# Gate and up as seven half-size block products, and the low part of weight tiles by an accumulating DMA

## Chip, cores and metric

One core of one Trainium2 chip runs the whole program in one launch. The metric is the device time of one execution in microseconds (us), median of several runs.

## What is computed

Two layers of a hybrid decoder for 512 prompt positions and 8 x 4 sample positions, 544 columns in all, in float32. In each layer four groups of heads read one projection of the normalised input, their outputs are joined by `w_out`, and a gated feed-forward part (FFN) follows. The change is about that part and about how all weights reach TensorE:

```
h2 = rmsnorm(x, p['norm2_g'])
gate, f_conv_new = causal_dwconv(st['f_conv'], h2 @ p['ffn_w_gate'], p['ffn_conv_w'])
x = x + (jax.nn.silu(gate) * (h2 @ p['ffn_w_up'])) @ p['ffn_w_down']
```

`D_MODEL` is 1024 (8 blocks of 128), `D_FF` is 2816 (22 blocks of 128), the convolution has width 3.

## The kernel before, in words

Activations lie with channels on the partitions and the 544 positions along the free dimension. A float32 product is made of three float32r products: a value is split into a high part (`hi`, a copy rounded to float32r) and a low part (`lo`, value minus `hi`), and `hi*hi`, `hi*lo` and `lo*hi` are added up in PSUM. `split` and `xsplit` do it for activations, `wprep` (L632) for weights.

**Weights.** `weights()` yields every weight tile in the order of use. `wload` loads the next one into a pool of two raw tiles (`wr`), a DMA on SP's queue (L630). `wprep` makes `wh` by a copy on ACT (L641) and `wl` by a subtraction on DVE (L643); both pools have three buffers. `wnext` keeps three tiles ready or in the making and hands out the oldest. A new `wh` can thus be written when PE has left a buffer that is three tiles older.

**Products.** `gemm` goes through the blocks of a tile: per block three products (high with high, weight high with activation low, weight low with activation high), each as two matmuls of 272 columns, so PE wants the low part of a tile at its fifth matmul. All matmuls are recorded at L417 by `mm`, which also keeps the planner's clock (`Order`): PE's order is fixed when the program is written, by that clock and the table `LAT` of waiting times for the side tasks; the order on the other engines is chosen by the scheduler of the tile framework.

**FFN.** `FGROUPS` cuts the 22 blocks of `D_FF` into groups of 6, 6, 6 and 4. For each block there is a gate product `pgt` and an up product `pup`, 8 blocks and 48 matmuls each. The gate result is multiplied by `rstd` (the norm), convolved (`conv`, a first pass on ACT at L694 and two on DVE), put through Silu on ACT, multiplied by `rstd` once more on POOL (L1584), then by the up result on DVE, and split into `hd`. POOL also copies the convolution's last columns to `sfo` (L1578, L1579). After a group come eight down products `pdn`, one per block of `D_MODEL`, that read the group's `hd` tiles and are added to `x`. The last two down products of the last layer are written out in `finale` as `pdl`, with one half of 272 columns at a time.

At the start of the program four weight tiles `w_tm` of 784 columns are the first that PE needs.

## Time and profile before

| | |
|---|---|
| median of 3 runs | 1375.87 us (1374.64 to 1376.35) |
| profiled execution, its own time | 1375.83 us |
| its span | 1374.0 us |
| PE busy | 1343.9 us, 98% |
| DVE, ACT, POOL busy | 777.2, 515.2, 292.2 us |
| DMA | 125.62 MB, mean 91 GB/s |
| granted TensorE clock, mean | 0.99 of 2.4 GHz |

The span runs from the first to the last instruction that the profiler saw; the execution's own time holds a little more around it. Busy times of different engines overlap. Durations of single matmuls overlap too, since they are pipelined: how fast PE goes is read from a run of them, as length over count.

### The profile page before, as it was taken

The page shows a single profiled execution, that of the slowest core. Times are in us where ns is not written, and L with a number is a line of the kernel's source. Part 1 is how long each engine was busy: PE and PEld are TensorE (multiplying, and loading weights), DVE is VectorE, ACT ScalarE, POOL GpSimd, SP SyncE. Part 2 cuts the span into 40 slices and gives each one's busy share as a digit, 9 for nine tenths or more (in the row PEclk, how much of TensorE's full clock was granted, in tenths as well). Part 3 has the DMA queues.
Part 4 walks back from the last instruction along what each step waited for, and adds up shares of the span by engine and source line. Part 5 has one row for each costly group of instructions (what it writes and reads, how often), then busy time and mean ns, then how long its engine had stood idle before and what let it go on. Part 6 is the DMA issues. An engine that isn't in the chain of part 4 may idle for free.

```text
span 1374.0 us, 30046 instructions
## 1 busy us (share of the span) xinstructions
PE 1343.9 (98%) x12982; PEld 1299.8 (95%) x12982; DVE 777.2 (57%) x1319; ACT 515.2 (37%) x852; POOL 292.2 (21%) x466
## 2 busy tenths in 40 slices
PE   8899999999999999999998999999999999999997
PEld 7888888999999999999998888989999999999997
DVE  5897944665445445435658977537444444444446
ACT  5446324443223223313534353335432332232234
POOL 2431220032103102203124311202320230121121
PEclk9899999999999999999999999999999999999999
DMA  6222241232232232232432222413223232322323
GB/s 224 89 83 72 82 133 43 82 113 77 81 106 79 76 107 80 74 106 67 140 120 79 78 82 62 138 52 87 92 81 89 93 85 80 98 89 71 103 68 96
DMA packets 48084, 125.62 MB, mean 91 GB/s; under 512 B 10144, under 2 KB 14432, under 8 KB 47824
## 3 DMA queue, kind: packets, MB, share of 16 engines
q1 hardware_dynamic: 47952, 123.70, 29.6%
q8 instruction: 102, 1.67, 0.5%
q14 instruction: 30, 0.25, 0.1%
HBM read 115.01 MB, written 8.67 MB: 90 GB/s over the span
## 4 chain that ended last, share of the span: by engine, by line
PE 88%; DVE 8%; issue 2%; ACT 1%; DMA 0%; DVEq 0%; SPq 0%; ACTq 0%
PE pup L417 19%; PE pgt L417 19%; PE pdn L417 19%; PE po L417 7%; PE ptm L417 2%; PE pj_b L417 2%; PE pj_z L417 2%; PE pj_u L417 2%; PE pj_h L417 2%; PE pj_cq L417 2%; PE pj_c L417 2%; PE p L417 2%; PE pj_v L417 1%; DVE wl L643 1%; DVE cacc L696 1%
## 5 line engine op out<-in xcount | busy, mean ns | idle before, releaser
L641 ACT ACTIVATE wh<-wr 128x1024 fp32r<-128x1024 f32 (+3 forms) x218 | 208.5, 957 | 502.0 <-PE pdn L417 177.2
L643 DVE TENSOR_TENSOR wl<-wr,wh 128x1024 fp32r<-128x1024 f32 (+3 forms) x218 | 246.2, 1129 | 24.2 <-ACT wh L641 18.3
L417 PE MATMUL pgt<-xl,wh 128*128 128x272 f32 x704 | 146.7, 290 | 0.0
L417 PE MATMUL pup<-xl,wh 128*128 128x272 f32 x704 | 146.7, 290 | 0.0
L417 PE MATMUL pup<-xh,wl 128*128 128x272 f32 x704 | 145.9, 289 | 0.0
L417 PE MATMUL pgt<-xh,wl 128*128 128x272 f32 x704 | 145.9, 289 | 0.0
L417 PE MATMUL pup<-xh,wh 128*128 128x272 f32 x704 | 145.9, 288 | 0.0
L417 PE MATMUL pgt<-xh,wh 128*128 128x272 f32 x704 | 145.9, 288 | 0.0
L417 PE MATMUL pdn<-hdl,wh 128*128 128x272 f32 x688 | 142.8, 289 | 0.0
L417 PE MATMUL pdn<-hdh,wh 128*128 128x272 f32 x688 | 142.4, 288 | 0.0
L417 PE MATMUL pdn<-hdh,wl 128*128 128x272 f32 x688 | 142.2, 288 | 0.0
L1600 DVE TENSOR_TENSOR xr<-xr,pdn 128x544 f32<-128x544 f32 x62 | 44.7, 721 | 142.0 <-PE pdn L417 141.8
L1578 POOL COPY sfo<-pbf 128x2 f32<-128x2 f32 x44 | 14.8, 336 | 517.9 <-DVE pbf L1576 517.9
L1576 DVE TENSOR_TENSOR pbf<-pgt,rstd 128x512 f32<-128x512 f32 x44 | 30.5, 693 | 148.3 <-PE pgt L417 142.9
L417 PEld LDWEIGHTS pgt<-xh,wh 128*128 128x128 f32 x704 | 110.8, 188 | 0.0
L417 PEld LDWEIGHTS pup<-xh,wh 128*128 128x128 f32 x704 | 110.8, 188 | 0.0
L417 PEld LDWEIGHTS pup<-xl,wh 128*128 128x128 f32 x704 | 110.7, 189 | 0.0
L417 PEld LDWEIGHTS pgt<-xl,wh 128*128 128x128 f32 x704 | 110.7, 189 | 0.0
L417 PEld LDWEIGHTS pgt<-xh,wl 128*128 128x128 f32 x704 | 110.7, 188 | 0.0
L417 PEld LDWEIGHTS pup<-xh,wl 128*128 128x128 f32 x704 | 110.7, 188 | 0.0
L417 PEld LDWEIGHTS pdn<-hdl,wh 128*128 128x128 f32 x688 | 108.1, 188 | 0.1
L417 PEld LDWEIGHTS pdn<-hdh,wl 128*128 128x128 f32 x688 | 108.1, 188 | 0.0
(523 smaller groups left out, 2680.0 us busy)
## 6 DMA issues: line engine op xcount, KB each, us to landing
wr<-w_g SPq DMA_DIRECT2D x44, 512.0 KB
wr<-w_u SPq DMA_DIRECT2D x44, 512.0 KB
wr<-w_ch SPq DMA_DIRECT2D x38, 512.0 KB
wr<-w_d SPq DMA_DIRECT2D x48, 384.0 KB
wr<-w_o SPq DMA_DIRECT2D x12, 384.0 KB
wr<-w_d SPq DMA_DIRECT2D x16, 256.0 KB
xr<-x_in SPq DMA_DIRECT2D x7, 544.0 KB
wr<-w_tm SPq DMA_DIRECT2D x8, 392.0 KB
```

Of the source, the lines that this page charges most:

```text
L417: nc.tensor.matmul(out, lhsT, rhs, **kw)
L641: act(hi, r, AF.Copy)
L643: tt(lo, r, hi.bitcast(F32), op=ALU.subtract)
L696: stt(acc[:, 0:out_n], pb[:, j:j + out_n], wcol[:, j:j + 1], acc[:, 0:out_n], op0=ALU.mult, op1=ALU.add)
L1576: tt(pb[:, 2:2 + SEQ], pflat(p, 0, SEQ), rstd[:, 0:SEQ], op=ALU.mult)
L1578: pool.tensor_copy(sfo[:, f, 0:2], pb[:, SEQ:SEQ + 2])
L1600: tt(xk(m), xk(m), pflat(p), op=ALU.add)
```

## The change

**Seven products for eight.** A gate and up pair is seen as a product of 2 x 2 blocks: outputs (gate, up) by halves of the 1024 input channels (4 blocks of 128 each), times those halves by halves of the 544 columns. Eight half-size block products become seven, on sums of weights and sums of activations. The first three pairs of a layer (`PLAIN`) stay as before, now with up right behind gate; in that time `Forms.make` builds the sums of activations, four times per layer: h2 times norm in `hn`, sums in `fu` and `fv`, and their high and low parts. The other 19 pairs run `seven`: chains of 4 blocks and 12 matmuls of 272 columns each, in the order `pA`, `pB`, `pD`, `pA`, `pD`, `pA`, `pC`. ACT copies parts of the chains' results out of PSUM between them (`sn`), DVE adds them up, and the second multiplication by `rstd` on POOL is gone for these pairs.

**Weight tiles of a pair.** Gate and up weights of a pair are loaded together into one raw tile `wg` of 2 x 1024 columns, a pool with one buffer. `wsums` makes `s31` and `s24` on DVE (one instruction of 1024 columns, two of 512). Four tiles go to PE: `g`, `s31`, `s24` (1024 columns each) and half of `u` (512 columns). The chains use g (twice), s31, s24 (twice), s31 again, u's half.

**Low part, for every weight tile of the program.** DVE's subtraction is replaced by: negate `hi` into `lo`, on DVE and ACT in turn (L729, L731 of the changed kernel), then a DMA that POOL issues and that adds the raw tile to `lo` (L732). There are 310 such DMAs.

**Order.** `FGROUPS` becomes 3, 5, 5, 5, 4. The down products of a group are spread behind the pairs of the next group, two behind each pair (three in the last group). Three times per layer a pair follows directly on a pair, at the borders of the groups. Several pools are merged into one, `slabs`; the sums for the second norm go from POOL to DVE.

```diff
-FGROUPS = [(0, 6), (6, 12), (12, 18), (18, 22)]
+FGROUPS = [(0, 3), (3, 8), (8, 13), (13, 18), (18, 22)]
+PLAIN = 3
...
+def _ffn_order():
+    o, todo = [], []
+    for f0, f1 in FGROUPS:
+        n = f1 - f0
+        for j, f in enumerate(range(f0, f1)):
+            o.append(("plain" if f < PLAIN else "seven", f, f0, f1))
+            k = -(-len(todo) // max(n - 1 - j, 1))
+            o += todo[:k]
+            todo = todo[k:]
+        o += todo
+        todo = [("down", m, f0, f1) for m in range(NK)]
+    return o + todo
+FFN_ORDER = _ffn_order()
...
-    hlp = ctx.enter_context(tc.tile_pool(name="hlp", bufs=28))
+    slabs = ctx.enter_context(tc.tile_pool(name="slabs", bufs=51))
...
+    wgu = ctx.enter_context(tc.tile_pool(name="wgu", bufs=1))
+    wsp = ctx.enter_context(tc.tile_pool(name="wsp", bufs=2))
...
-                pool.tensor_tensor(a, a, b, op=ALU.add)
+                self.es[0].tensor_tensor(a, a, b, op=ALU.add)
...
+    class Forms:
+        def __init__(self, src):
+            self.src, self.got, self.b11 = src, [], None
+        def make(self, kp):
+            h = []
+            for k in (kp, kp + NK // 2):
+                x, g = self.src(k)
+                t = n5("hn", T)
+                stt(t, x, g, rstd, op0=ALU.mult, op1=ALU.mult)
+                h.append(t)
+            (b11, b12), (b21, b22) = ((t[:, 0:HT], t[:, HT:T]) for t in h)
+            u, v = n5("fu", T), n5("fv", T)
+            n1, n2, t3, n4 = u[:, 0:HT], u[:, HT:T], v[:, 0:HT], v[:, HT:T]
+            tt(n1, b11, b12, op=ALU.subtract)
+            stt(n2, n1, -1.0, b22, op0=ALU.mult, op1=ALU.subtract)
+            tt(t3, b22, b12, op=ALU.subtract)
+            tt(n4, b21, n2, op=ALU.add)
+            j = kp % 2
+            if j == 0:
+                self.b11 = [nx("f1" + c, [128, T], F32R) for c in "hl"]
+            c_ = slice(HT * j, HT * j + HT)
+            act(self.b11[0][:, c_], b11, AF.Copy)
+            tt(self.b11[1][:, c_], b11, self.b11[0][:, c_].bitcast(F32), op=ALU.subtract)
+            sb, su, sv = split(h[1], "f2"), split(u, "f3"), split(v, "f4")
+            a, b = slice(0, HT), slice(HT, T)
+            self.got.append([[(t[0][:, s], t[1][:, s]) for t, s in
+                              ((self.b11, c_), (sb, a), (sb, b), (su, a), (su, b), (sv, a), (sv, b))]])
+        def parts(self):
+            return [[g[0][i] for g in self.got] for i in range(7)]
...
+    def chain(o, wt, k0, xs, start=True):
+        hi, lo = wt
+        n = len(xs)
+        for k in range(n):
+            xh, xl = xs[k]
+            for i, (w, x) in enumerate(((hi, xh), (hi, xl), (lo, xh))):
+                mm(o, w[:, k0 + k, :], x, start=start and k == 0 and i == 0, stop=k == n - 1 and i == 2,
+                   skip_group_check=not start)
+            yield 0.0
...
+            for kind, i, f0, f1 in FFN_ORDER:
+                if kind == "down":
+                    yield I["w_d"][l, i, :, f0:f1], f1 - f0, 128
+                elif kind == "plain":
+                    yield I["w_g"][l, i], NK, 128
+                    yield I["w_u"][l, i], NK, 128
+                else:
+                    yield I["w_g"][l, i], I["w_u"][l, i]
...
+        if len(x) == 3:
             r = wrp.tile([128, x[1], x[2]], F32, tag="wr", name="wr")
             nc.sync.dma_start(r, x[0])
-            wload_.append(r)
+        else:
+            r = wgu.tile([128, 2, NK, 128], F32, tag="wg", name="wg")
+            for i, src in enumerate(x):
+                nc.sync.dma_start(r[:, i], src)
+        wload_.append(r)
...
+    def wsums(gu):
+        K = NK // 2
+        g, u = gu[:, 0], gu[:, 1]
+        s31 = wsp.tile([128, NK, 128], F32, tag="ws", name="s31")
+        s24 = wsp.tile([128, NK, 128], F32, tag="ws", name="s24")
+        q = gu.rearrange("p a (h k) f -> p (a h) (k f)", h=2)
+        tt(s31.rearrange("p (h k) f -> p h (k f)", h=2), q[:, 0:4:3], bc(q[:, 2], 1, 2), op=ALU.add)
+        tt(s24[:, 0:K], g[:, 0:K], s31[:, K:NK], op=ALU.add)
+        tt(s24[:, K:NK], g[:, K:NK], s24[:, 0:K], op=ALU.add)
+        return [g, s31, s24, u[:, K:NK]]
...
+        if not wsplit_:
+            if not wload_:
+                wload()
+            if not wload_:
+                return
+            r = wload_.pop(0)
+            wsplit_.extend([r] if len(r.shape) == 3 else wsums(r))
+        r = wsplit_.pop(0)
         nk, w = r.shape[1], r.shape[2]
         hi = whp.tile([128, nk, w], F32R, tag="wh", name="wh")
         act(hi, r, AF.Copy)
         lo = wlp.tile([128, nk, w], F32R, tag="wl", name="wl")
-        tt(lo, r, hi.bitcast(F32), op=ALU.subtract)
+        turn[0] ^= 1
+        if turn[0]:
+            ts(lo, hi.bitcast(F32), -1.0, None, op0=ALU.mult)
+        else:
+            act(lo, hi.bitcast(F32), AF.Copy, scale=-1.0)
+        pool.dma_start(out=lo, in_=r, accum_op=ALU.add)
         wready.append((hi, lo))
...
-            nrm = Norm((pool, pool))
+            nrm = Norm((dve, dve))
...
+            def seven(f):
+                B11, B21, B22, N1, N2, T3, N4 = fm.parts()
+                K = NK // 2
+                a_ = ps("pA", [128, HT])
+                b_ = psa.tile([128, HT], F32, tag="pa1", name="pB")
+                d_ = psa.tile([128, HT], F32, tag="pa0", name="pD")
+                sn = pd.tile([128, 4, HT], F32, tag="d5", name="sn")
+                pb, dec = gate_in(f)
+                n = SEQ - HT
+                wg_ = wnext()
+                yield from chain(a_, wg_, 0, B11)
+                act(sn[:, 0], a_, AF.Copy)
+                yield from chain(b_, wg_, K, B21)
+                tt(pb[:, 2:2 + HT], b_, sn[:, 0], op=ALU.add)
+                w31 = wnext()
+                yield from chain(d_, w31, K, N1)
+                act(sn[:, 1], d_, AF.Copy)
+                w24 = wnext()
+                yield from chain(a_, w24, 0, N2, start=False)
+                act(sn[:, 2], a_, AF.Copy)
+                yield from chain(d_, w24, K, B22, start=False)
+                tt(pb[:, 2 + HT:2 + SEQ], d_[:, 0:n], sn[:, 2, 0:n], op=ALU.add)
+                tt(dec[:, :, 2:6], bs(d_[:, n:HT]), bs(sn[:, 2, n:HT]), op=ALU.add)
+                sl = gate_out(f, pb, dec)
+                yield from chain(a_, w31, 0, T3, start=False)
+                act(sn[:, 3], a_, AF.Copy)
+                up = n5("up", T)
+                stt(up[:, HT:T], a_, -1.0, sn[:, 1], op0=ALU.mult, op1=ALU.subtract)
+                c_ = psmm("pC")[:, 0:HT]
+                yield from chain(c_, wnext(), 0, N4)
+                tt(up[:, 0:HT], c_, sn[:, 3], op=ALU.subtract)
+                tt(sl, sl, up, op=ALU.mult)
+                hid[f] = split(sl, "hd")
...
+            for kind, i, f0, f1 in FFN_ORDER:
+                if kind == "plain":
+                    for step in plain(i, i == 0):
+                        yield step
+                    if i < 2:
+                        fm.make(2 * i)
+                        fm.make(2 * i + 1)
+                    continue
...
```

On ACT, in the FFN of layer 0, a stretch of one pair and the tiles behind it. Before (`wh` is a weight tile's high part, `hdh` that of a hidden block, `cacc` the convolution, `sl` Silu):

```order
L641 ACTIVATE wh_4642<-wr_4640 128x768
L694 ACTIVATE cacc_4631<-pbf_4624,prm0_125 128x560
L1582 ACTIVATE sl_4635<-cacc_4631 128x512
L1583 ACTIVATE sl_4635<-cacc_4631 128x32
L641 ACTIVATE wh_4702<-wr_4700 128x768
L499 ACTIVATE hdh_4695<-sl_4635 128x544
```

After (`wl` is the negation, `sn` a copy out of PSUM; `wh_5667` and `wh_5726` are the two down tiles, `wg_5750` the next pair's raw tile):

```order
L725 ACTIVATE wh_5616<-s24_5532 128x1024
L731 ACTIVATE wl_5618<-wh_5616 128x1024
L1696 ACTIVATE sn_5612<-pA_5609 128x272
L725 ACTIVATE wh_5647<-wg_5528 128x512
L1701 ACTIVATE sn_5612<-pD_5611 128x272
L1704 ACTIVATE sn_5612<-pA_5609 128x272
L725 ACTIVATE wh_5667<-wr_5665 128x640
L783 ACTIVATE cacc_5701<-pbf_5613,prm0_122 128x560
L731 ACTIVATE wl_5669<-wh_5667 128x640
L725 ACTIVATE wh_5726<-wr_5724 128x640
L1710 ACTIVATE sn_5612<-pA_5609 128x272
```

The negation of `s24` and of the first down tile now stand on ACT, the latter behind the convolution's first pass.

On POOL in the same stretch, before (`sfo` and `pbf` are the convolution's edges):

```order
L1578 COPY sfo_3909<-pbf_5106 128x2
L1579 COPY sfo_3909<-pbf_5106 128x16
L687 MEMSET pbf_5236 128x2
L689 COPY pbf_5236<-stf_3907 128x8x2
L1584 TENSOR_TENSOR sl_5117<-sl_5117,rstd_104 128x544
```

After:

```order
L732 DMA wl_5618<-s24_5532 128x1024
L732 DMA wl_5649<-wg_5528 128x512
L1656 COPY sfo_3941<-pbf_5613 128x2
L1657 COPY sfo_3941<-pbf_5613 128x16
L732 DMA wl_5669<-wr_5665 128x640
L776 MEMSET pbf_5835 128x2
L778 COPY pbf_5835<-stf_3939 128x8x2
L732 DMA wl_5728<-wr_5724 128x640
L732 DMA wl_5760<-wg_5750 128x1024
```

Six DMAs per pair and its two down tiles stand in POOL's queue, with the copies of the convolution's edges between them.

On PE, the border between a pair and the first down product after the change (a name with DMASW is the end of an accumulating DMA):

```order
L436 MATMUL pC_5723<-f4l_4312,wh_5647 128x272
L436 MATMUL pC_5723<-f4h_4311,wl_5649 128x272
L436 MATMUL pdn_5749<-hdh_4587,wh_5667 128x272 [waits DVE_49,Activation_49]
L436 MATMUL pdn_5749<-hdh_4587,wh_5667 128x272
L436 MATMUL pdn_5749<-hdl_4588,wh_5667 128x272 x2
L436 MATMUL pdn_5749<-hdh_4587,wl_5669 128x272 [waits DMASW5_49]
L436 MATMUL pdn_5749<-hdh_4587,wl_5669 128x272
```

The fifth matmul of a down product waits for the accumulating DMA into its low part, where it waited for DVE.

## Rows read from the trace of the kernel before

**Rows 1.** The page, its first part: busy time, share of the span, instructions.

```profile
span 1374.0 us, 30046 instructions
PE 1343.9 (98%) x12982; PEld 1299.8 (95%) x12982; DVE 777.2 (57%) x1319; ACT 515.2 (37%) x852; POOL 292.2 (21%) x466
```

**Rows 2.** The chain that ended last, merged: start us, length us, what.

```profile
304.05 6.08 PE pup L417 x48
...
358.77 36.37 PE pdn L417 x288
...
1357.46 4.53 PE pdl L417 x36
```

**Rows 3.** Windows, FFN of layer 0: first two gate and up groups.

```profile
core 0: us, PE busy (x) PEld busy (x) DVE busy (x) ACT busy (x) POOL busy (x), PEclk, DMA share, GB/s
285.00:359.00 74.00, 74.00 (x587) 74.00 (x586) 36.78 (x50) 29.46 (x43) 22.42 (x32) 1.00 0.26 84
395.00:468.00 73.00, 73.00 (x579) 73.00 (x578) 35.42 (x47) 24.70 (x36) 20.32 (x30) 1.00 0.28 83
```

**Rows 4.** Lines by form, PE and its weight loads, one product of three.

```profile
L417 PE MATMUL pup<-xh,wl 128*128 128x272 f32 x704 | 145.9, 289 | 0.0
L417 PEld LDWEIGHTS pup<-xh,wl 128*128 128x128 f32 x704 | 110.7, 188 | 0.0
```

**Rows 5.** Lines by form, ACT and DVE: shapes, count | busy us, mean ns | idle before.

```profile
L641 ACT ACTIVATE wh<-wr 128x1024 fp32r<-128x1024 f32 x132 | 139.6, 1058 | 313.9 <-PE pgt L417 142.1 <-PE pdn L417 63.9 <-PE pup L417 27.3
L641 ACT ACTIVATE wh<-wr 128x768 fp32r<-128x768 f32 x60 | 50.7, 846 | 156.0 <-PE pdn L417 105.4 <-PE pgt L417 26.0 <-PE pup L417 18.7
L694 ACT ACTIVATE cacc<-pbf,prm 128x560 f32<-128x560 f32 x44 | 33.7, 765 | 7.0 <-DVE pbf L1577 4.5
L641 ACT ACTIVATE wh<-wr 128x512 fp32r<-128x512 f32 x18 | 11.4, 632 | 26.6 <-PE pgt L417 8.7 <-PE pup L417 6.2 <-PE pdn L417 5.7
...
L643 DVE TENSOR_TENSOR wl<-wr,wh 128x1024 fp32r<-128x1024 f32 x132 | 167.9, 1272 | 19.8 <-ACT wh L641 13.9
L643 DVE TENSOR_TENSOR wl<-wr,wh 128x512 fp32r<-128x512 f32 x18 | 12.3, 684 | 0.0
```

**Rows 6.** Timeline, 394.9 to 397.6 us, one weight tile on ACT, DVE and SP's queue.

```profile
394.93 1.06 ACT L641 ACTIVATE wh<-wr 128x1024 fp32r<-128x1024 f32 x1 [3.49 <-PE pdn L417]
...
396.02 1.23 DVE L643 TENSOR_TENSOR wl<-wr,wh 128x1024 fp32r<-128x1024 f32 x1
...
397.27 0.33 SPq L630 DMA_DIRECT2D wr<-w_g  x1
```

**Rows 7.** Windows of half a microsecond behind that issue; last columns: DMA share, GB/s.

```profile
398.00:398.50 0.50, 0.50 (x6) 0.50 (x5) 0.00 (x0) 0.00 (x0) 0.00 (x0) 1.00 0.56 66
...
399.50:400.00 0.50, 0.50 (x6) 0.50 (x5) 0.00 (x0) 0.00 (x0) 0.00 (x0) 1.00 1.06 434
400.00:400.50 0.50, 0.50 (x6) 0.50 (x5) 0.00 (x0) 0.00 (x0) 0.00 (x0) 1.00 0.15 57
400.50:401.00 0.50, 0.50 (x6) 0.50 (x5) 0.00 (x0) 0.00 (x0) 0.00 (x0) 1.00 0.00 0
```

**Rows 8.** Lines, POOL: the same copy in the FFN and elsewhere.

```profile
L1579 POOL COPY sfo<-pbf 128x16 f32<-128x16 f32 x44 | 44.2, 1003 | 0.0
...
L1503 POOL COPY sbo<-pbb 128x16 f32<-128x16 f32 x4 | 0.8, 195 | 0.0
```

**Rows 9.** Timeline, 5.8 to 8.0 us: the program's first weight tile.

```profile
5.89 0.84 ACT L641 ACTIVATE wh<-wr 128x784 fp32r<-128x784 f32 x1
...
6.77 0.98 DVE L643 TENSOR_TENSOR wl<-wr,wh 128x784 fp32r<-128x784 f32 x1 [0.51 <-ACT wh L641]
...
7.80 0.45 PE L417 MATMUL ptm<-wl,xh 128*128 128x392 f32 x1 [0.57 <-DVE wl L643]
```

**Rows 10.** Windows at 50 to 60 us, columns as in rows 3.

```profile
50.00:55.00 5.00, 0.74 (x4) 0.74 (x4) 4.90 (x15) 2.46 (x4) 1.85 (x6) 0.77 0.13 49
55.00:60.00 5.00, 5.00 (x24) 5.00 (x24) 4.19 (x10) 2.35 (x5) 0.00 (x0) 0.50 0.33 107
```

**Rows 11.** The page, DMA queues: packets, MB, share of 16 engines' span.

```profile
q1 hardware_dynamic: 47952, 123.70, 29.6%
```

More of the change, by code (lines that the diff above doesn't have):

```diff
@@ L451, in n5, with nx @@
         return p5.tile([128, w], F32, tag="w5", name=nm)
-    def nx(nm, shape):
-        return px.tile(shape, F32, tag="x5", name=nm)
+    def nx(nm, shape, dt=F32):
+        return slabs.tile(shape, dt, tag="s5", name=nm)
     def ncc(nm, shape):
@@ L459, in ny @@
     def ny(nm, shape):
-        return pyy.tile(shape, F32, tag="y5", name=nm)
+        return nx(nm, shape)
     def ps(nm, shape):
@@ L496, in split @@
     def split(src, nm):
-        hi = hlp.tile([128, T], F32R, tag="hl", name=nm + "h")
-        lo = hlp.tile([128, T], F32R, tag="hl", name=nm + "l")
+        hi, lo = nx(nm + "h", [128, T], F32R), nx(nm + "l", [128, T], F32R)
         act(hi, src, AF.Copy)
@@ L543, in xsplit @@
     def xsplit(x, g):
-        hi = hlp.tile([128, T], F32R, tag="hl", name="xh")
-        lo = hlp.tile([128, T], F32R, tag="hl", name="xl")
+        hi, lo = nx("xh", [128, T], F32R), nx("xl", [128, T], F32R)
         act(hi, x, AF.Copy, scale=g)
@@ L615, in weights @@
                 yield I["w_o3"][l, m], NK, 128
[L616 to L621 removed]
+            for kind, i, f0, f1 in FFN_ORDER:
[6 more added lines that the diff above has]
+                    yield I["w_g"][l, i], I["w_u"][l, i]
     wgen = weights()
[L624 removed]
+    wload_, wsplit_, wready, turn = [], [], [], [0]
     def wload():
         x = next(wgen, None)
[L628 removed]
+        if x is None:
+            return
+        if len(x) == 3:
             r = wrp.tile([128, x[1], x[2]], F32, tag="wr", name="wr")
             nc.sync.dma_start(r, x[0])
[L631 to L638 removed]
+        else:
[13 more added lines that the diff above has]
+        return [g, s31, s24, u[:, K:NK]]
+    def wprep():
+        if not wsplit_:
+            if not wload_:
+                wload()
+            if not wload_:
+                return
+            r = wload_.pop(0)
+            wsplit_.extend([r] if len(r.shape) == 3 else wsums(r))
+        r = wsplit_.pop(0)
         nk, w = r.shape[1], r.shape[2]
@@ L786, in gates @@
         L.beta, L.nbeta, L.gg, L.ex, L.bec = beta, nbeta, gg, ex, bec
-        L.oT = [lv.tile([128, T], F32, tag=f"oT{pr}", name=f"oT{pr}") for pr in range(2)]
+        L.oT = [nx(f"oT{pr}", [128, T]) for pr in range(2)]
         od.mark(f"gates{l}", 1.0)
     def halves(x):
-        h = hlp.tile([128, SEQ], F32R, tag="hl", name="hvh")
-        lo = hlp.tile([128, SEQ], F32R, tag="hl", name="hvl")
+        h, lo = nx("hvh", [128, SEQ], F32R), nx("hvl", [128, SEQ], F32R)
         act(h, x, AF.Copy)
@@ L1442, in main @@
             cq = L.cq = pd.tile([128, 2, T], F32, tag="d5", name="cq")
-            ck = L.ck = lv.tile([128, T], F32, tag="ck", name="ck")
+            ck = L.ck = nx("ck", [128, T])
             rope = pd.tile([128, 2, T], F32, tag="d5", name="rope")
@@ new lines, in main, with gate_in, gate_out @@
+            hid = {}
+            fm = Forms(lambda k: (xk(k), P(l, "n2g", k, k + 1)))
+            def gate_in(f):
+                pb = n5("pbf")
+                return pb, conv_in(pb, 3, stf[:, f])
+            def gate_out(f, pb, dec):
+                pool.tensor_copy(sfo[:, f, 0:2], pb[:, SEQ:SEQ + 2])
+                pool.tensor_copy(sfo[:, f, 2:18].rearrange("p (b s) -> p b s", b=DB), dec[:, :, 4:6])
+                acc, accd = conv(pb, 3, P(l, "fcw", 3 * f, 3 * f + 3), 560)
+                sl = n5("sl", T)
+                act(sl[:, 0:SEQ], acc[:, 0:SEQ], AF.Silu)
+                act(bs(sl[:, SEQ:T]), accd, AF.Silu)
+                return sl
@@ new lines, in plain @@
+            def plain(f, first):
+                p = psmm("pgt")
+                yield from gemm(p, wnext(), xs)
+                pu = psmm("pup")
+                gu = gemm(pu, wnext(), xs)
+                if first:
+                    for _ in range(4):
+                        yield next(gu)
+                    nrm.finish()
+                pb, dec = gate_in(f)
+                tt(pb[:, 2:2 + SEQ], pflat(p, 0, SEQ), rstd[:, 0:SEQ], op=ALU.mult)
+                tt(dec[:, :, 2:6], bs(pflat(p, SEQ, T)), bs(rstd[:, SEQ:T]), op=ALU.mult)
+                sl = gate_out(f, pb, dec)
+                pool.tensor_tensor(sl, sl, rstd, op=ALU.mult)
+                yield 0.0
+                yield from gu
+                tt(sl, sl, pflat(pu), op=ALU.mult)
+                hid[f] = split(sl, "hd")
+                yield 0.0
@@ new lines, in main @@
+            for kind, i, f0, f1 in FFN_ORDER:
[6 more added lines that the diff above has]
+                    continue
+                if kind == "seven":
+                    yield from seven(i)
+                    continue
+                m, last = i, f1 == NF
+                hd = [hid[f] for f in range(f0, f1)]
+                if last and l + 1 == depth and m >= NK - 2:
+                    if m == NK - 2:
+                        yield from finale(xk, xr, nnrm, hd)
+                    continue
+                p = psmm("pdn")
+                yield from gemm(p, wnext(), hd)
+                tt(xk(m), xk(m), pflat(p), op=ALU.add)
+                if last:
+                    if l + 1 < depth:
+                        nx_xs.append(xsplit(xk(m), P(l + 1, "n1g", m, m + 1)))
+                    nnrm.feed(m, xk(m))
+                    if l + 1 == depth:
+                        act(xk(m), xk(m), AF.Copy, scale=fng[:, m:m + 1])
+                yield 0.0
```

70 lines of the change are left out of this document (5 added, 65 removed).

## The prediction

> **What bounds the kernel now.** I read the page's first part, then the chain of waits, the windows by stage, the lines by form, and last the timeline around one weight tile. PE is busy for 1343.9 of 1374.0 us [rows 1], and the chain is a string of PE pieces: a gate or up product of 48 matmuls takes 6.08 us, eight down products of 36 take 36.37 us [rows 2]. Both give 0.1267 us per matmul. In the feed-forward (FFN) stretches PE never stops, while DVE, ACT and POOL are busy for 35.42, 24.70 and 20.32 of 73 us [rows 3]. So in the FFN only two things count: how many matmuls PE issues, and whether a weight tile is ever late.
>
> A weight tile is made well ahead. Its first copy on ACT starts when PE leaves the buffer three tiles back, at 394.93; the subtraction on DVE is done at 397.25 [rows 6]. PE wants the tile two tiles later, 12.2 us after the start. 2.3 us are used, so some 10 us are in hand.
>
> **What is saved.** A gate and up pair is 96 matmuls now. Seven chains of 4 blocks x 3 products are 84. Each matmul already loads its own weights (704 loads for 704 matmuls [rows 4]), so a chain that uses a weight for one half only loses nothing there, and the pace holds where a product fills a single 272-wide tile: 36 matmuls in 4.53 us [rows 2]. Twelve matmuls fewer are 1.52 us, for 19 of 22 pairs in 2 layers: 38 x 1.52 = 58 us less. That gain I count as certain.
>
> **What is added: a transfer inside the making of every tile.** The low part was one DVE instruction (1272 ns for 1024 columns [rows 5]). It becomes a negated copy, on DVE and ACT in turn, and an accumulating DMA that POOL issues. No row of before shows such a DMA. Call D the time from POOL reaching it to the low part being usable, for 1024 columns.
> - Lower bound: a plain load of the same 524 KB. SP issues it at 397.27 [rows 6]; bytes flow from about 398.2, at up to 434 GB/s, and only 28 KB are left after 400.0 [rows 7]: landed at 400.1, D = 2.8 (0.9 lead, 1.9 body). No reason excludes less, so that is a rival below.
> - Upper bound: that load twice over, 5.6, since source and destination are both read.
> - I take the load plus one more reading at its peak rate, 524 KB / 434 GB/s = 1.2: D = 4.0. It is nearest to the row of the load, with the one thing added that the operation must do. By columns (lead 0.9, rest in proportion): 2.8 for 640, 2.5 for 512, 3.3 for 784.
>
> The Trainium skill ("DMA: Bandwidth & Descriptors", section "Anatomy of one DMA — SWDGE (gpsimd) path") fits a DMA issued from GpSimd as 2.0 us plus bytes over 436e3, which is an estimate of 3.2 us for this tile. With it in place of 4.0 the sum below would be 1435; no run here shows an accumulate, so it stays beside the sum.
>
> **Where D lands on the path.** Three buffers remain, but a pair of 84 matmuls now uses four tiles (g, s31, s24, half of u), so a tile lasts PE 1.52 or 3.04 us instead of 6.08. The look-ahead shrinks to the following, per pair and the two down products behind it. PE needs 10.64 us for the pair and 3.80 for each 5-block down product.
> - *s24.* Its buffer comes free when the down product ahead of the pair ends. PE reaches its low part after three chains and two matmuls: 4.56 + 0.25 = 4.8 us. The work: ACT copy 1.06, ACT negation 1.06 (same form [rows 5]), 0.1 of hand-overs, D 4.0: 6.2. **Late by 1.4 us.**
> - *First down tile.* It takes the buffer that s24 leaves after its second chain; PE is there after two more chains and four matmuls: 3.04 + 0.51 = 3.55 us. The work: copy of 640 columns 0.74 (between 632 ns for 512 and 846 for 768), then on ACT's queue the convolution's 0.77 stands before the negation of 0.74 [rows 5], 0.1, and 2.8: 5.15. **Late by 1.6 us.**
> - *Covered.* s31 has two down products' end and two chains ahead (3.80 + 3.04 + 0.25 = 7.1 us against 1.06 + 1.27 + 4.0); u's half four chains (6.3 against 3.8); the second down tile the whole first one; the next g both down products.
>
> So a pair saves 1.52 and waits 3.0: +1.5 us, for 32 of the 38 pairs: **+48 us**.
>
> *Pair directly behind pair* (3 per layer, at the group borders). The raw tile for g and u has one buffer. Its next load can start only when the accumulate of u's half has read it: two chains 3.04, copy 0.63, negation 0.68 (512 columns at the DVE price of a two-input op [rows 5], an upper bound), hand-over 0.1, 2.5: 6.95 us into the pair. The load takes 2.8, copy and negation 2.1, D 4.0, 0.1: 16.0, where PE wants it at 10.9. Late by 5.1, then s24 by 1.4: 6.5 less 1.5 saved, +5.0 x 6 = **+30 us**.
>
> *Start.* The first low part follows its copy by 0.98 us on DVE and PE takes it at once [rows 9]. It will be 0.85 for the negation plus 3.3: +3.2 on each of the first three tiles, before PE has anything else: **+10 us**.
>
> *New operands.* Four times per layer DVE and ACT make the sums of activations: per time one half-width and three full copies on ACT, some 2.4 us, about 10 per layer, queued before the copies of weight tiles while only plain pairs cover them. Their lead of 10 us absorbs most; I take half, 5 per layer: **+10 us**.
>
> At nothing: DVE's three weight sums per pair (1272 + 2 x 684 ns [rows 5]) lie between load and use in slack of the down products; the removed multiplication by the norm on POOL, the removed subtractions and the moved norm sums were off the chain. If DVE lost its slack, s31 would be late next.
>
> **Sum.** The profiled execution took 1375.83 us, its span 1374.0; the median of the runs is 1375.87, so the two agree. The 58 us are inside the net figures: 48 + 30 + 10 + 10 = +98, **1474 us**. With D = 2.8 the same steps give -13 + 11 + 7 + 10 = +15, 1391. With 5.6: 131 + 53 + 13 + 10 = +207, 1583.
>
> **Rivals.**
> 1. *The accumulate is quick and the saving stays: faster.* The point is D = 2.5; below it the waits cost less than 1.52 per pair. At D = 2.0 s24 is on time, the first down tile late by 0.4, pair behind pair by 2.0: -36 + 3 + 5 + 10 = -18, 1358. For it: no byte goes to HBM, and rate peaks at 434 GB/s. Against: a load with no second operand takes 2.8 [rows 6, 7]. Chance 0.09.
> 2. *POOL is held up at the issue.* POOL's copy of 16 columns takes 1003 ns in the FFN, 195 ns for the same shape elsewhere [rows 8]: something on the other engines holds it for 0.8 us. If an issue is held for half of that, 0.4 at each wait: 0.8 x 32 + 1.2 x 6 = +33, 1507. Chance 0.12. The Trainium skill ("SBUF — State Buffer", section "SBUF: two separate sides") names a shared DVE and GpSimd port that a DVE op of the two-port kind, as the negation may be, takes for a whole instruction, and says GpSimd can then not write descriptors; the 0.8 us fits a lock, while no row shows one on an issue.
> 3. *The DMA engines become the bound.* A pair with two down products loads 1.70 MB and accumulates 2.49 MB. 123.70 MB in 29.6% of the span [rows 11] is 304 GB/s while busy: 5.6 us for loads, and at two passes 16.4 for accumulates, 22.0 against the 21.2 of my sum, close to the edge already. At two and a half passes, 26: +4.9 x 32 = +157 more, 1631. For peak-rate bytes (434) the total is 15.4, which speaks against. Chance 0.10.
> 4. *Gain and waits cancel*, D near 2.5: 1376. Chance 0.02.
>
> The forecast has the remaining 0.67. A further cost in the range only: after 4.3 us of idle PE in 5 the granted clock showed 0.50, the 1.2 GHz level, over the next window [rows 10]; waits of 1.5 us are short of that, those of 5 are not.
>
> **How the numbers follow.** The range runs from 1390 (D = 2.8) to 1600 (D = 5.6 and a little clock): it leaves out rivals 1, 3 and 4, 0.21 together. Slower by over 0.2% (2.75 us, about what a measurement of this kernel can tell from no change): forecast and rivals 2 and 3, 0.89; within it rival 4, 0.02; faster rival 1, 0.09.
>
> **What would show it.** Right: PE's matmuls drop by 38 x 12 and its busy time by some 55 us, yet PE idles in the FFN on low parts, 1 to 2 us at each pdn behind a pC and at the third chain of a pair, 5 at the g of a pair behind a pair; ACT and POOL lie on the chain. An accumulate that lands under 2.5 us, or an FFN stretch without idle PE, makes it wrong; so does DMA busy near 1.0 in FFN windows (rival 3).

## The result, and the profile after

The changed kernel takes **1880.8 us** (1874.3 to 1884.0, 4 runs) against 1376.0 on the same chip: 1.367 times the time of before, 95% interval 1.363 to 1.370. The forecast was 1474, its range ended at 1600. The direction was right, the size was not. In an execution now and then the chip falls into a slower state; the ratios leave such executions out, which matters for one of the four of `before_acc16k` below.

The page of the changed kernel, parts 1 to 4, beside [rows 1] and [rows 11] of before:

```profile
span 1878.1 us, 30986 instructions
...
PE 1457.5 (78%) x12526; PEld 1371.8 (73%) x12526; DVE 819.6 (44%) x1596; ACT 774.3 (41%) x1283; POOL 428.3 (23%) x722
...
q0 software_dynamic: 44640, 130.63, 36.1%
q1 hardware_dynamic: 50256, 123.70, 21.1%
...
PE 34%; DMA 28%; issue 21%; DVE 8%; ACT 6%; POOL 2%; SPq 0%; DVEq 0%; POOLq 0%; ACTq 0%
```

PE has 456 matmuls fewer (12526 for 12982), and yet is busy 114 us longer. It also stands still for 421 us of the span instead of 30. The chain, a string of PE pieces before [rows 2], is now 34% PE, 28% DMA and 21% "issue" (time in which an engine waited for nothing that the profile shows). The windows of the FFN of layer 0, columns as in [rows 3], show both losses at once:

```profile
480.00:530.00 50.00, 33.34 (x216) 32.04 (x217) 17.20 (x30) 19.75 (x31) 10.36 (x18) 0.86 0.56 121
530.00:580.00 50.00, 36.97 (x244) 35.45 (x242) 19.26 (x32) 20.51 (x31) 9.54 (x16) 0.86 0.65 152
```

PE idles for a quarter to a third of the time, its granted clock falls from 1.00, the 2.4 GHz level, to a mean of 0.86 between that and 1.2 GHz, and the DMA engines are far from full (0.56, 0.65). What does PE wait for? Its waits, longest groups (us in total, times, longest):

```profile
PE pdn L436 <- DMA wl<-wr: 118.1, 53, 4.8
PE pA L436 <- DMA wl<-s: 111.6, 38, 4.7
PE pA L436 <- DMA wl<-wg: 67.4, 30, 5.5
PE pD L436 <- DMA wl<-s: 41.3, 26, 2.4
```

Low parts, all of them: of down tiles (`pdn`), of s24 (`pA` from `s`), of g (`pA` from `wg`) and of s31 (`pD`). The prediction had named the first two, g only where a pair follows directly on a pair, and had called s31 covered; the half of u, called covered too, is not in the list. POOL's timeline for one pair and its two down tiles (start us, length, instruction, idle time before it and what ended it) tells why:

```profile
536.26 0.87 POOL L732 DMA_DIRECT2D wl<-wr  x1 [3.92 <-DVE up L1712]
541.43 0.87 POOL L732 DMA_DIRECT2D wl<-wg  x1 [4.30 <-issue]
546.83 0.87 POOL L732 DMA_DIRECT2D wl<-s  x1 [4.53 <-issue]
551.55 0.86 POOL L732 DMA_DIRECT2D wl<-s  x1 [3.85 <-issue]
556.30 0.89 POOL L732 DMA_DIRECT2D wl<-wg  x1 [3.89 <-issue]
...
561.56 0.87 POOL L732 DMA_DIRECT2D wl<-wr  x1 [1.61 <-ACT wl L731]
...
566.60 0.89 POOL L732 DMA_DIRECT2D wl<-wr  x1 [3.93 <-DVE up L1712]
```

An issue takes POOL 0.87 us, and then POOL sits for some 4 us before the next although nothing in the trace holds it ("issue"). The chain shows the transfer of 551.55:

```profile
551.55 4.44 DMA wl<-s
```

It lands at 555.99, and the next one starts at 556.30. By the landing times in the trace not one of the 310 accumulates is issued before the one ahead of it has landed; the closest follows 0.31 us behind. Six of them make the period: 536.26 to 566.60, 30.3 us, where the prediction had 21.2. Of it 26.6 us are transfers; for 2.0 us, from 559.53 to 561.56, the queue is empty until ACT has negated the first down tile.

### The profile page after: what moved, and what is told of

It reads as the page before. It is cut to its first block, busy times and chain, and to the rows that moved or that the text cites. A ratio compares the mean times of both kernels' runs of the same rounds, so it can differ in the third digit from the quotient of the medians.

```text
span 1878.1 us, 30986 instructions
## 1 busy us (share of the span) xinstructions
PE 1457.5 (78%) x12526; PEld 1371.8 (73%) x12526; DVE 819.6 (44%) x1596; ACT 774.3 (41%) x1283; POOL 428.3 (23%) x722
## 3 DMA queue, kind: packets, MB, share of 16 engines
q0 software_dynamic: 44640, 130.63, 36.1%
## 4 chain that ended last, share of the span: by engine, by line
PE 34%; DMA 28%; issue 21%; DVE 8%; ACT 6%; POOL 2%; SPq 0%; DVEq 0%; POOLq 0%; ACTq 0%
DMA wl<-wr 9%; DMA wl<-s 9%; PE pdn L436 7%; PE pD L436 4%; PE pA L436 4%; DMA wg<-w_u 3%; ACT wh L725 3%; POOL wl L732 2%; PE pup L436 2%; DMA wl<-wg 1%; PE pj_z L436 1%; PE pj_b L436 1%; DMA wr<-w_d 1%; PE po L436 1%; PE pj_h L436 1%
## 5 line engine op out<-in xcount | busy, mean ns | idle before, releaser
L732 POOL DMA_DIRECT2D wl<-wr x158 | 139.7, 884 | 555.0 <-ACT wl L731 161.4
L725 ACT ACTIVATE wh<-wr 128x1024 fp32r<-128x1024 f32 (+5 forms) x158 | 131.1, 829 | 199.5 <-PE pD L436 48.8
L725 ACT ACTIVATE wh<-s 128x1024 fp32r<-128x1024 f32 x76 | 80.4, 1057 | 150.8 <-PE pdn L436 137.5
L731 ACT ACTIVATE wl<-wh 128x1024 fp32r<-128x1024 f32 (+5 forms) x155 | 137.2, 885 | 2.9
L732 POOL DMA_DIRECT2D wl<-s x76 | 67.4, 887 | 309.6 <-issue 204.2
L436 PEld LDWEIGHTS pdn<-hdh,wh 128*128 128x128 f32 x688 | 127.9, 222 | 6.2 <-ACT hdh L516 2.8
L732 POOL DMA_DIRECT2D wl<-wg x76 | 66.5, 875 | 280.3 <-issue 226.5
L729 DVE TENSOR_SCALAR wl<-wh 128x1024 fp32r<-128x1024 f32 (+5 forms) x155 | 94.2, 608 | 65.0 <-ACT wh L725 61.0
L436 PE MATMUL pA<-f1h,wl 128*128 128x272 f32 x152 | 52.6, 346 | 67.6 <-DMA wl<-wg 67.4
L725 ACT ACTIVATE wh<-wg 128x1024 fp32r<-128x1024 f32 x76 | 64.1, 843 | 79.8 <-PE pB L436 43.9
L785 DVE SCALAR_TENSOR_TENSOR cacc<-pbf,prm,cacc 128x560 f32<-128x560 f32 x88 | 70.5, 801 | 34.0 <-ACT cacc L783 32.8
```

What stands on the lines that cost most here:

```text
L436: nc.tensor.matmul(out, lhsT, rhs, **kw)
L725: act(hi, r, AF.Copy)
L729: ts(lo, hi.bitcast(F32), -1.0, None, op0=ALU.mult)
L731: act(lo, hi.bitcast(F32), AF.Copy, scale=-1.0)
L732: pool.dma_start(out=lo, in_=r, accum_op=ALU.add)
L785: stt(acc[:, 0:out_n], pb[:, j:j + out_n], wcol[:, j:j + 1], acc[:, 0:out_n], op0=ALU.mult, op1=ALU.add)
```

## The experiments

The text on record before the runs uses letters. A: the accumulates run one at a time, because the descriptor space (`dynamic_dma_scratch_size=512`, a line of the changed kernel that the diff ahead of the prediction does not show; the kernel before leaves it at its default) has room for one. B: the throughput of the DMA engines. C: single tiles made too late. D stands in the first runs for what seven products cost by themselves, in later ones for raw tiles held by the accumulate. All verdicts are ratios to the kernel before on the same chip.

### Room for descriptors

`space2048`: the space 512 to 2048 bytes, 51 slabs to 50 to make room. `space512`: the slab alone. `acc16k`: 16384 bytes, 43 slabs (a slab is one buffer in the merged pool of activations).

```diff
-    slabs = ctx.enter_context(tc.tile_pool(name="slabs", bufs=51))
+    slabs = ctx.enter_context(tc.tile_pool(name="slabs", bufs=50))
-    nc = _bacc.Bacc(..., dynamic_dma_scratch_size=512)
+    nc = _bacc.Bacc(..., dynamic_dma_scratch_size=2048)
```

> The changed kernel with one buffer less in the pool of activations (50 for 51), descriptor space for POOL's DMAs left at 512 bytes. Control for the next run. Every theory: the buffer does not matter, 1850 to 1910 us, POOL idle some 500 us before its accumulating DMAs.

> The same with 2048 bytes of descriptor space. Theory A (one in flight): in the trace of the change POOL starts an accumulating DMA when the one before has landed, since 512 bytes hold the descriptors of one; with four times the space several are under way, POOL's 525 us of idle go, a pair with its two down products falls from 30.4 us to 21 to 23, and the time to 1470 to 1600 us. Theory B (engines): accumulates are slow on the DMA engines and would wait for each other there; space changes nothing, 1850 to 1910 us, with each DMA landing later behind its issue. Theory C (my prediction's: only single late tiles) would give 1474 in both and is already off.

> The changed kernel with 16384 bytes of descriptor space in place of 512, and 43 activation slabs instead of 51 to make room. Theory A (the accumulating DMAs run one at a time because the space holds the descriptors of one; the 310 of them, at 3.2 to 6.6 us each, add up to some 1390 us of a queue that stands still at every gap): POOL no longer sits before an issue for want of space (204 + 227 us of 'issue' in the changed kernel), accumulates overlap, and what is left over the seven products with a subtraction (1436) is the longer making of single tiles: 1480 to 1580 us. Rival B (the DMA engines' throughput: two transfers that overlap each take longer): landing of 512 KB rises from 4.4 towards 8 us and the time stays where 2048 bytes left it, 1640 to 1700.

Measured: 1897.2 (a single run) for the slab alone, **1681.2** with 2048 bytes (ratio 1.223, 1.220 to 1.227), **1658.6** with 16384 (1.205, 1.203 to 1.207). POOL's wait for nothing shown, in the changed kernel and with 2048 bytes:

```profile
POOL wl L732 <- issue: 525.3, 138, 7.7
```

```profile
POOL wl L732 <- issue: 55.2, 22, 7.0
```

The room is worth 200 us with 2048 bytes and some 220 with 16384, and the wait that it explains is gone but for a tenth; up to three accumulates are now under way at once. So A is shown as a cause, but as the whole it missed both numbers: some 220 us over the subtracting kernel below remain even with 16384 bytes. The time of `acc16k` is the one that B had named (1640 to 1700), but not for B's reason: 512 KB out of `s` still land after 4.4 us and not towards 8, and the engines' share in the two windows above is 0.72 and 0.68.

### The parts of the change alone

`seven_sub`: seven products, the subtraction put back. `before_acc512`: the kernel before with negation and accumulate.

```diff
-        turn[0] ^= 1
-        if turn[0]:
-            ts(lo, hi.bitcast(F32), -1.0, None, op0=ALU.mult)
-        else:
-            act(lo, hi.bitcast(F32), AF.Copy, scale=-1.0)
-        pool.dma_start(out=lo, in_=r, accum_op=ALU.add)
+        tt(lo, r, hi.bitcast(F32), op=ALU.subtract)
```

> Seven products kept, low parts by DVE's subtraction again, no accumulating DMA. Theories A and B: both put the loss in the accumulates, so PE's 456 matmuls fewer show and the waits for DMA go: 1330 to 1430 us, PE busy 1290 to 1310. Theory D (the seven products themselves, their order, sums and three buffers, cost the time): over 1500 us.

> The kernel before with the accumulating DMA alone, 512 bytes of space. Theory A: a tile lasts PE 6.08 us in a gate or up product and 4.56 in a down product of six blocks, one DMA after the other takes about 5.3 (0.9 to issue, 4.4 to land) and 4.7, so nearly hidden: 1390 to 1470 us, most of the loss at the start and in the projections. Theory B: much the same here, 1400 to 1500. Were an accumulate simply too late whatever the order, over 1550.

Measured: **1436.1** (1.043, 1.041 to 1.045) and **1510.2** (1.098, 1.097 to 1.100). The parts alone cost 60 and 134 us, together 505. A likely reason, argued and not tested by itself, is that they multiply each other's demands: the seven products turn 218 low parts into 310 and leave PE less work over each. Both numbers are misses, upward: the first lies 6 us above the range of A and B, the second 40 above A's and 10 above B's. In `seven_sub` PE waits for DVE at the down products (for `up` 30.9 us, for `xr` 24.8), hardly for low parts (5.5 at `pD`). In `before_acc512` ACT waits for loads of raw tiles, where its copies had waited for PE [rows 5]:

```profile
ACT wh L641 <- DMA wr<-w_u: 190.1, 43, 6.9
ACT wh L641 <- DMA wr<-w_d: 177.2, 59, 6.0
```

The subtraction let go of a raw tile 2.3 us after its copy began [rows 6]; an accumulate reads it until it has landed, so the next load starts that much later (SP waits 1230.9 us for accumulates in `before_acc16k`).

### Two locks in the kernel before

`before_acc16k`: 16384 bytes. `before_acc_raw4`: four raw buffers (`wrp`) instead of two, 4096 bytes. `before_acc_raw4_512`: four raw buffers, 512 bytes.

```diff
-    wrp = ctx.enter_context(tc.tile_pool(name="wrp", bufs=2))
+    wrp = ctx.enter_context(tc.tile_pool(name="wrp", bufs=4))
```

> The kernel before with its low parts made as in the change (negated copy, accumulating DMA), with 16384 bytes of descriptor space where the same edit with 512 bytes took 1510. A: a tile there has some 10 us in hand and the making takes 2.1 + 4 to 6, so with the accumulates free to overlap the time goes back to 1380 to 1420. B (throughput of the DMA engines): 1460 to 1510, as before.

> The kernel before with the accumulating low parts and room for several descriptors (4096 bytes), and four buffers for raw weight tiles instead of two. With two buffers and 16384 bytes it took 1501, and SP waited 1231 us for accumulates before it could load the next raw tile. Theory D (the accumulate keeps the raw tile until it has landed, so that load, copy, negation and accumulate of one buffer form a loop of some 13 us for a tile, 6.5 each with two buffers, against the 6.08 that PE takes): with four buffers the loop is off the path and the time is 1380 to 1420. Rival B (the DMA engines: loads and accumulates that overlap slow each other, whatever the buffers): 1470 to 1510.

> The kernel before with accumulating low parts and four raw buffers (1380 with 4096 bytes), with 512 bytes of descriptor space, one accumulate at a time. Its 218 accumulates at 4 to 6 us are some 1200 us of queue in all, under the 1376 of PE, and in the feed-forward part one of 512 KB (4.5 to 6 us) for 6.08 us of PE: the queue just keeps up. A with that reckoning: 1380 to 1420. If one at a time costs by itself in every kernel: 1460 to 1510.

Measured: 1501.0 (four runs from 1488.0 to 1512.5; 1.088, 1.082 to 1.094) with room alone, 1501.0 (1.092, 1.089 to 1.096) with raw buffers alone, **1380.3** (1.004, 1.002 to 1.005) with both. Two of the three were misses of A as the single reason: either limit alone keeps nearly the whole cost. The first number lay in B's range, but the engines' throughput is not what set it, since four raw buffers bring the time to 1380.3 with the same transfers. In the kernel with both, ACT waits for PE's buffers again and no longer for loads:

```profile
ACT wh L641 <- PE pgt L417: 170.3, 44, 5.0
ACT wh L641 <- PE pdn L417: 157.4, 61, 3.8
```

With raw buffers alone, 512 KB land after 6.1 us, issue included, and follow each other every 6.4 to 7.7 us (539.44, 545.87, 552.44, 560.13, 566.70 on POOL): just over the 6.08 that PE needs for a product [rows 2]. POOL's waits for "issue" are 360 us there. That a queue "just keeps up" was reckoned with 4.5 to 6 us for each.

### More buffers in the changed kernel

`acc_raw`: 4096 bytes, two buffers for `wg`, four for `wr`, 41 slabs. `acc_b4`: 2048 bytes, two for `wg`, four instead of three for `wh` and `wl`, 42 slabs, and down products spread over all pairs of a group (`max(n - j, 1)` for `max(n - 1 - j, 1)`), so that no pair follows directly on a pair. `acc_b4_512`: the same with 512 bytes.

> The changed kernel with 4096 bytes of descriptor space, two buffers for the gate and up tile instead of one and four for the other raw tiles instead of two (41 activation slabs to make room); three buffers for high and low parts as before. D (raw tiles held by accumulates set the 1659 that 16384 bytes left): 1490 to 1560, that is the 1436 of the subtracting kernel and the longer making of single tiles. B (the engines): 1610 to 1670. C (the making of single tiles behind three high and low buffers is late by itself, as the prediction had it, with 4.4 to 5.7 us of landing instead of 4.0 and the lost clock): also 1600 to 1660, told from B by landing times that stay near 4.4.

> The subtracting kernel that took 1347.6 (four buffers for high and low parts, two for the gate and up tile, spread down products) with its low parts made as in the change, 2048 bytes of descriptor space and 42 slabs. C (what is left in the accumulating kernel with more raw tiles, 1605, is the making of single tiles behind three high and low buffers): one buffer more gives every tile a product or two (1.5 to 3.8 us) more, which covers waits of 1.5 to 3 us and not those of 5: 1400 to 1500. B (throughput of the DMA engines) or the order of work on POOL's and ACT's queues, which the buffers do not touch: 1540 to 1610.

> The same with 512 bytes of descriptor space (43 slabs): against the 1347.6 it is one edit, subtraction to negation and accumulate. One at a time, six accumulates of some 4.4 to 5.1 us in a pair with its down products are a queue of 28 to 30 us whatever the buffers (theory A): 1780 to 1880. If buffers could cover it: under 1600.

Measured: **1605.2** (1.168, 1.165 to 1.170), **1526.5** (1.110, 1.108 to 1.112) and **1883.2** (1.369, 1.367 to 1.371). The last is the time of the changed kernel: while the accumulates run one at a time, none of these buffers helps.

`acc_raw` is 53 us below `acc16k`, so the raw tiles that accumulates hold (D) were a part and not the whole. Its time is in C's range, and its landing time says C too: 4.5 us out of `s`, with the engines at 0.72 and 0.67 in the first two windows shown. PE's waits in it are those of single tiles:

```profile
PE pdn L436 <- DMA wl<-wr: 91.7, 32, 5.6
PE pA L436 <- DMA wl<-s: 53.1, 31, 3.7
PE pA L436 <- DMA wl<-wg: 28.4, 9, 5.1
...
PE pD L436 <- DMA wl<-s: 9.7, 10, 1.8
```

These are the places that the prediction had named. Its own sums for them are 1.6 x 32 = 51 us for down tiles, 1.4 x 38 = 53 for s24, 5.1 x 6 = 31 for g and nothing for s31. Its mechanism is in the kernel, then, and comes to light once one at a time is lifted; how near two of the sizes come is luck in part, since D was taken too small.

With the same 2048 bytes, the buffers and the spread order of `acc_b4` are worth 155 us together (1681.2 to 1526.5), less than C had said (1400 to 1500) and more than B. The rest shows in the windows of `acc_b4` (last columns: clock, DMA share, GB/s):

```profile
530.00:580.00 50.00, 46.31 (x329) 45.66 (x330) 24.86 (x43) 26.49 (x43) 14.43 (x22) 0.90 0.87 190
580.00:630.00 50.00, 45.26 (x340) 44.04 (x339) 23.18 (x39) 26.74 (x41) 17.07 (x26) 0.97 0.91 214
```

Now the 16 DMA engines are nearly full, up to four accumulates are under way at once, and 512 KB out of `s` land after 7.2 us instead of 4.4.

### The addition

`copy512` and `copy_b4`: the changed kernel and `acc_b4` with a plain copy in place of the accumulate.

```diff
-        pool.dma_start(out=lo, in_=r, accum_op=ALU.add)
+        pool.dma_start(out=lo, in_=r)
```

> The changed kernel with the accumulating DMA replaced by a plain copying DMA of the same tile on the same queue, so the low part is not formed: the addition is left out of the computation. It prices the addition. If the second reading of the destination costs the 1.2 us of 4.0 that the prediction gave it, a 512 KB transfer lands after 3.2 to 3.6 us instead of 4.4, and with 310 of them in a row the time falls by 250 to 370 us to 1510 to 1630. If the addition costs nothing and the copy from SBUF to SBUF is itself so slow, landing stays at 4.2 to 4.6 and the time at 1840 to 1890.

> The kernel with every buffer widened (1526, where the 16 DMA engines were busy for 0.87 to 0.91 of the feed-forward windows), its accumulating DMA replaced by a plain copying DMA of the same bytes: the addition is left out of the computation, negations, queue, order and buffers stay. If the DMA engines' time on the accumulate is what remains (B): in the changed kernel with copies the same 130.63 MB took 371 us of 16 engines' time (24.6% of 1507.6) instead of 678 (36.1% of 1878), so the engines' share in those windows falls to 0.6 or less and the time to 1360 to 1420. If the extra copy on ACT, the negation and the order on POOL's queue are what remains: 1480 to 1526.

Measured: 1509.4 (1.097, 1.095 to 1.099) and **1363.3** (0.991, 0.990 to 0.993). The page's DMA parts, first the changed kernel's, then that of `copy512`: POOL's queue (packets, MB, share of 16 engines; the former stands above), and the issues out of `s` (count, KB each, median us to landing):

```profile
wl<-s POOLq DMA_DIRECT2D x76, 512.0 KB, 4.4
```

```profile
q0 software_dynamic: 44640, 130.63, 24.6%
...
wl<-s POOLq DMA_DIRECT2D x76, 512.0 KB, 2.9
```

The addition adds 1.5 us to a landing of 2.9, and for the same 130.63 MB takes 678 us of the 16 engines (36.1% of 1878.1) for 371 (24.6% of 1507.6): 1.83 times. The time between the changed kernel and `copy512` (1880.8 to 1509.4) is not the price of the addition alone: with the same 512 bytes, copies are not held to one at a time. By their landing times 96 of the 310 are issued before the one ahead has landed, and POOL's wait of 525.3 us is down to

```profile
POOL wl L732 <- issue: 69.6, 28, 5.1
```

Why the space holds more of them, no run shows. `copy_b4` is the cleaner test, since `acc_b4` has room as well. In it the engines' share in the two windows above is 0.71 and 0.72 and PE is busy for 49.76 and 50.00 us:

```profile
530.00:580.00 50.00, 49.76 (x396) 49.41 (x395) 26.90 (x46) 30.79 (x48) 10.67 (x26) 1.00 0.71 231
580.00:630.00 50.00, 50.00 (x401) 50.00 (x400) 29.37 (x52) 32.87 (x51) 12.88 (x31) 1.00 0.72 237
```

The time came out as B had it, the share of engines not (0.6 or less was expected). Of the 179 us between `acc_b4` and the subtracting kernel with nearly the same buffers (1347.6, below; one slab more), 163 are the addition; negations, copying DMAs, POOL's order and the second copy are in the other 16. Whether the addition costs by the engines' time or by each tile's later landing, this edit does not separate, as it lowers both. The Trainium skill ("Collectives: The Full Stack", section "The bandwidth ceiling: the fold count and why AG ≠ RS ≠ AR") says of ReduceScatter that its add needs two source reads through one ring and so runs at about half the rate of AllGather, which copies: a measured ratio of 1.93. The 1.83 here is near it; how the engines read, no run here shows.

### A version that beats both

`v7`: `seven_sub` with four `wh` and `wl`, spread down products, and the weight sums on POOL. `v9`: the sums back on DVE. `v9g2`: two buffers for `wg` as well (43 slabs).

```diff
-    wgu = ctx.enter_context(tc.tile_pool(name="wgu", bufs=1))
-    whp = ctx.enter_context(tc.tile_pool(name="whp", bufs=3))
-    wlp = ctx.enter_context(tc.tile_pool(name="wlp", bufs=3))
+    wgu = ctx.enter_context(tc.tile_pool(name="wgu", bufs=2))
+    whp = ctx.enter_context(tc.tile_pool(name="whp", bufs=4))
+    wlp = ctx.enter_context(tc.tile_pool(name="wlp", bufs=4))
...
-            k = -(-len(todo) // max(n - 1 - j, 1))
+            k = -(-len(todo) // max(n - j, 1))
```

> Seven products with the subtraction on DVE and no accumulate, and three edits against what they lost: four buffers for high and for low parts (47 slabs), the sums of weight tiles on POOL, and the down products spread so that no pair follows directly on a pair. If the 60 us that the seven products lost came from the shorter look-ahead of three buffers and DVE's queue, the 58 us of saved matmuls come through: 1335 to 1375. Rival (PE waits for the sums of activations and for hidden states, which these edits don't touch): 1390 to 1440.

> Seven products with subtraction, four buffers for high and low parts and spread down products, the sums of weight tiles back on DVE. In the kernel with the sums on POOL, DVE's subtraction of 1024 columns took 2.32 us beside a POOL sum where it takes 1.22 alone, and 28.9 us of idle PE waited for DVE. If that contention cost it: 1355 to 1390. Rival (DVE's own queue is too long with the sums on it): 1400 to 1430.

> The same with two buffers for the gate and up tile (43 slabs instead of 47), so that its load does not wait for the last use of the tile before. If late loads still cost something: 5 to 25 us less than with one buffer; if loads are covered, the same within 5 us.

Measured: 1399.5 (1.018, 1.016 to 1.020), 1369.9 (0.996, 0.995 to 0.997), **1347.6** (0.980, 0.979 to 0.982): 28 us faster than before. `v7` to `v9` and `v9` to `v9g2` are one edit each (the slabs apart); what four buffers and the spread order are worth singly was not run. The sums on POOL were a miss for a reason of their own. DVE by form, with the sums on POOL, then on DVE:

```profile
L780 DVE SCALAR_TENSOR_TENSOR cacc<-pbf,prm,cacc 128x560 f32<-128x560 f32 x88 | 115.9, 1317 | 3.6 <-ACT cacc L778 2.6
...
L727 DVE TENSOR_TENSOR wl<-wg,wh 128x1024 fp32r<-128x1024 f32 x38 | 77.6, 2042 | 7.3 <-ACT wh L725 7.3
```

```profile
L780 DVE SCALAR_TENSOR_TENSOR cacc<-pbf,prm,cacc 128x560 f32<-128x560 f32 x88 | 69.9, 795 | 1.9 <-ACT cacc L778 1.8
...
L727 DVE TENSOR_TENSOR wl<-wg,wh 128x1024 fp32r<-128x1024 f32 x38 | 46.3, 1218 | 0.2
```

The same instructions take 1.66 and 1.68 times as long on DVE when POOL adds tiles beside them, and DVE lies on the path to the down product: PE waits 28.9 us for `up` in `v7`, 14.2 in `v9`.

## Why the prediction was wrong

- **What bounds before; 58 us saved.** Right in the count (456 matmuls), and PE is busy for 55.5 us less in `v9g2` (1288.4 for 1343.9). "Certain" it was not: with three buffers and one `wg` the seven products lost 60 us even with the subtraction. The prediction followed the low part alone; DVE's queue was at nothing, and it makes PE wait for `up` and `xr` (55.7 us in `seven_sub`), which are not weight tiles at all.
- **D = 4.0.** Near for 512 KB out of `s` (4.4), too small for the others: 5.1 for g's 512 KB, 4.3 for a down tile's 320 KB (taken as 2.8), 3.2 for 256 KB of u (taken as 2.5), and 5.7 for 512 KB of other raw tiles, just over the upper bound of 5.6. That the addition adds 1.5 to a copy's 2.9 fits the reason given, one more reading (1.2); that it is a reading is not shown. The Trainium skill's fit ("DMA: Bandwidth & Descriptors", section "Anatomy of one DMA — SWDGE (gpsimd) path": 2.0 us plus bytes over 436e3, an estimate of 3.2 us) is near the plain copy, 2.9, and not the accumulate.
- **Where D lands: the step that failed.** D was put behind each tile's own copy and negation as a latency, and its waits were listed tile by tile ("Late by 1.4", "Late by 1.6", the rest "Covered"). That takes the queue to be free whenever a negation is done. The accumulates share one queue that held one at a time, so D is an occupancy: six in 30.3 us where the sum had 21.2. A pair with no down products behind it has four, and takes 19.4 to 21.6 us where the reckoning gives 10.64 + 6.5 = 17.1: some 5.1 us for each accumulate in both cases. A check was at hand: the prediction's own D for the six, 3 x 4.0 + 2.5 + 2 x 2.8 = 20.1 us, already nearly fills 21.2. By that D alone one at a time would still have fitted; each also took some 5.1 us where D has 3.4 on average. The tiles called covered are late too: PE waited 41.3 us for s31 (at `pD`) and 67.4 for g.
- **Where the 407 us between forecast and result lie.** From the first `pA` of a layer to its last `pC` the trace has 553.0 and 550.6 us, where the reckoning gives 379 (19 x 10.64, 109 of down products, 67 of waits): 345 of the 407. The last eight down products of the two layers have some 30, the plain pairs 20, and the program outside the FFN 11.
- **Clock.** "A little clock" in the range only. The waits of up to 5 us took the granted clock to 0.86 in the FFN and 0.90 over the span; PE's busy time rose by 114 us with 456 matmuls less. In the one-at-a-time kernel this is hardly a sum on top, since the pairs go at the pace of the queue, 5.1 us for each accumulate; how much it is elsewhere was not separated. How PE's busy time grows with a lower clock shows without that queue in `acc_raw`: at a mean granted clock of 0.94 PE is busy for 1372.1 us, in `v9g2` with the same matmuls, at 0.985, for 1288.4.
- **New operands.** No run undoes the sums of activations alone. The three plain pairs of a layer take 44.8 us in `seven_sub` in place of six products of 6.08, 36.5: 8 more, where 5 had been taken.
- **Start, +10.** About right: PE waits 16.5 us for accumulates before `ptm` in five places, where it waited 2.8 for the split before.
- **Rivals.** The quick accumulate did not come. POOL was held at the issue, but by the descriptor room, not by DVE. The DMA engines were not the bound (0.56 to 0.65), nor with room alone (about 0.7); with room and buffers they are nearly full (0.87 to 0.91), so the third rival points at what comes last. Its price for the six accumulates of a pair, 16.4 us of the engines, was high: 2.49 MB at the 130.63 MB in 678 us above are 12.9. What the prediction lacked was the rival that one line of the kernel, the size of the descriptor space, lets nothing overlap.

The whole, as a ladder of the kernels above: 1347.6 with a subtraction, 1363.3 with negation and copying DMA, 1526.5 with the addition, 1605.2 with three high and low buffers and pairs behind pairs (and four raw buffers and 4096 bytes, for two and 2048), 1658.6 with the raw buffers of the change (and 16384 bytes), 1681.2 with 2048 bytes, 1880.8 as it is. Most rungs change more than one thing; single edits are 1363.3 to 1526.5 (the addition) and 1681.2 to the 1897.2 of `space512` (the room).

## What to carry to other kernels

Ask of every transfer that a change adds to a loop how long it occupies its queue, not only how long it takes: multiply by the number in a period, and look for what lets two of them be under way at once. A transfer that reads a buffer also holds it, so each stage in front needs a buffer more, and removing one such limit alone may show nothing. Fewer matmuls pay only if the tiles that feed them are as early as before.

## What the runs showed of the hardware

- 512 bytes of descriptor space let one accumulate of 192 to 512 KB be under way, POOL standing at the next for some 4 us; with 2048 those waits fall from 525 to 55 us. Of plain copies of the same tiles, 512 bytes let more than one be under way (96 of 310 overlap the one ahead).
- An accumulating DMA of 512 KB within SBUF lands 4.4 us after POOL begins its issue, a copying one after 2.9; the accumulate takes 5 to 7 when up to four are under way (`acc_b4`). POOL's issue takes 0.88 us for the one and 0.54 for the other.
- DVE's two-input instructions take up to 1.68 times as long, as a mean, when POOL adds weight tiles beside them (`v7` against `v9`). The Trainium skill ("SBUF — State Buffer", section "SBUF: two separate sides") describes a port pair shared by the two, which a DVE instruction with two SBUF inputs and a GpSimd one that reads SBUF take from each other for a whole instruction. The rows are in line with it; a lock as such they do not show.
